# A hybrid encoder layer on one core: a projection moved into the attention stage, and every third low part made in PSUM and copied by ScalarE

## The chip, the cores and the metric

The kernel runs on one core of a Trainium2 chip. Its metric is the device time of one execution in microseconds (us). Three runs of the kernel before took 3136.9, 3138.69 and 3145.14 us; the median is 3138.69. One further execution was profiled. The engines are named as in the profile: PE does matmuls (PEld is its loading of weights), DVE is the vector engine, ACT the scalar engine, POOL GpSimd, SP the engine on whose queue nearly all DMAs are issued.

## The reference

The input `x` is 2048 rows of 1024 numbers in float32. The layer is cut here to its data flow:

```python
h = layer_norm(x) @ w_in                     # 1024 -> 9 x 1024
q, k, v, z_sb, c_val, c_gate, z_cv, g_sb, g_cv = split(h)
o_sb = stick_breaking_attention(q, k, v)     # 16 heads of 64, strictly causal
y_sb = (o_sb * silu(z_sb)) @ w_sb_proj
u = c_val * sigmoid(c_gate)
u = causal_depthwise_conv(u, conv_w) + conv_b        # 31 taps per channel
u = silu(layer_norm(u))
y_cv = (u * silu(z_cv)) @ w_cv_proj
merged = sigmoid(g_sb) * y_sb + sigmoid(g_cv) * y_cv
out = layer_norm(2 ** 0.25 * x + merged @ w_out)
```

The attention's weight of key s for query t is `sigmoid(l_ts)` times the product of `1 - sigmoid(l_tj)` over the keys j between them, so a running product over the keys stands where another attention has a softmax.

## The kernel before, in words

All matmuls that matter run in the type fp32r. A float32 operand is split for them into a high part (an ACT copy to fp32r, L116) and a low part (a DVE subtraction, L117); a product of two split operands takes three matmuls, high by high, high by low and low by high. A tile is 128 partitions by 512 columns (`CH`); the sequence has four chunks of 512, in two halves h = 1 (chunks 3 and 2) and h = 0 (chunks 1 and 0). The rows are reversed on the host, so half 1 is the first half in time of the attention's keys that both need.

There are three phases.

1. **First phase.** The input's layer norm and transposes, and 56 groups of projections by `w_in` (L909), each with seven products instead of eight. `order(h)` sets the groups' order. The groups `u` give the convolution's input; the convolution itself is a queue `slow` of single steps on DVE (its taps are L409). `slow_step` is called once per filling piece. It adds `PACES[phase]` to a balance and, if the balance is at least 1, takes one off and does one step.
2. **Attention stage.** For 8 head pairs, 2 heads and 4 query blocks of 256: two logits matmuls into PSUM (`lg`, L583 and L584), a sigmoid on ACT (`nb`, L586), a running product on DVE (the scan, L589), transposes on PE into a PSUM tile `tp` (L612, `turn`), the split of `tp` into `th` and `tl` (L116 and L117), and products of `v` with `th` and `tl` added up in `pv` (L628). There are 576 such tiles. `weave_attention` writes their order: the `pv` of a tile stands two turns behind its transposes. Between these items stand pieces of filling work, six matmuls each (L201), spread in proportion to the attention's estimated costs: the projections of half 0 for q, k, v and z, and the output projections `branch("s", 1)` (by `w_sb`) and `branch("c", 1)` (by `w_cv`). The convolution's mean and layer norm (`conv_mean`, `conv_ln`, L447 to L505) are delayed entries in the same list of pieces. `END` is how many entries of the list are left for after the attention.
3. **Tail.** `branch("s", 0)`, the output rows of chunks 3 and 2 (L1243), `branch("c", 0)`, the output rows of chunks 1 and 0.

PE's order is the order in which the code is written. On ACT, DVE and SP a scheduler places instructions by priority at build time; each engine then runs its list strictly in order. `tp` has two PSUM buffers, `th` and `tl` two buffers each, `nb` four.

The weights `w_sb` and `w_cv` are loaded and split by `load_w` once for each half. A block's weights are requested during the block before it.

Of the kernel before, what the change touches and what calls it, by code (L numbers as in the profile page):

```python
# [8 lines left out]
F32 = mybir.dt.float32  # L9
# [4 lines left out]
P = 128  # L14
# [16 lines left out]
PACES = [0.78, 1.25, 0.6]  # L31
# [4 lines left out]
END = 14  # L36
W0 = 3
N1 = 2
# [16 lines left out]
def layer_kernel(ctx: ExitStack, tc, x, w_in, w_sb, w_cv, w_out, vecs, cw, rows, out):  # L55
# [15 lines left out]
    nc.gpsimd.memset(ones, 1.0 / D)  # L71
    vec = const.tile([P, 5, KB], F32, name="vec")
# [9 lines left out]

    mhalf = const.tile([P, 1], F32, name="mhalf")
# [60 lines left out]
    def load_w(src, col):  # L144
# [3 lines left out]
        for g in range(2):  # L148
# [7 lines left out]
            split(raw, hi[:, ks], lo[:, ks])  # L156
        return hi, lo
# [282 lines left out]
    def conv_mean(h):  # L440

        def mean(c):
            while len(convs) < (2 - h) * KB:
                slow_step(True)
            ps, mu, ys = mm_p.tile([P, CH], F32, name="mm"), st(), st()
            dma(ys.rearrange("p (e n) -> p e n", e=2), ysd[h][:, :, c % 2 * 256:c % 2 * 256 + 256])
# [3 lines left out]
        return [lambda c=c: mean(c) for c in half(h)]  # L450

    def conv_ln(c):
# [11 lines left out]
        def s2(m):  # L464
# [8 lines left out]
            else:  # L473
                nc.vector.tensor_tensor(out=box["sq"], in0=box["sq"], in1=y, op=ALU.add)

# [4 lines left out]
        def m2():  # L480
            ps = mm_p.tile([P, CH], F32, name="mm")
            for b in range(nb):
                nc.tensor.matmul(ps[:, b:b + 1], lhsT=box["sq"][:, b * P:(b + 1) * P], rhs=ones[:, 0:1], start=True, stop=True)
            v = sm.tile([P, nb], F32, name="var", bufs=2)
            nc.vector.tensor_copy(out=v, in_=ps[:, :nb])
# [3 lines left out]
        def m3():  # L489
            ps = mm_p.tile([P, CH], F32, name="mm")  # L490
            rb = st()
            nc.vector.tensor_copy(out=rb.rearrange("p (b r) -> p b r", b=nb), in_=box["v"].unsqueeze(2).to_broadcast([P, nb, P]))
            for b in range(nb):
                nc.tensor.matmul(ps[:, b * P:(b + 1) * P], lhsT=rb[:, b * P:(b + 1) * P], rhs=ident, start=True, stop=True)
# [14 lines left out]
        return ([m1] + wait + [(lambda m=m: s2(m)) for m in range(KB)] + wait + [m2] + wait + [m3]  # L509
# [3 lines left out]
    def attention(at, kv, lg_p, pv_p):  # L513
# [5 lines left out]
        sums = {}  # L519
# [38 lines left out]
        def make_step(i, a, qc, lo, hi, diag, last, k2, v2, qd, ql, po, prev, load):  # L558
# [39 lines left out]
            for t in range(nt):  # L598
                box = {}

                def turn(t=t, box=box):
# [3 lines left out]
                    for sb in (1, 0):  # L605
                        off = t * 256 + sb * P
                        o0 = at_
                        for j in range(2):
# [3 lines left out]
                            nc.tensor.transpose(out=tp[:, at_:at_ + P], in_=tiles[j][:, so:so + P], identity=ident)  # L612
# [3 lines left out]
                    tl = at.tile([P, CH], F32R, name="tl", bufs=2)  # L616
                    with tc.high_priority(offset=500):
# [700 lines left out]
```

## Time and profile before

| | |
|---|---|
| median of 3 runs | 3138.69 us |
| profiled execution, its own time | 3146.49 us |
| its span, first to last instruction | 3144.7 us |
| mean granted clock of PE | 0.978 |
| PE busy, matmuls | 2896.8 us (92%) x14666 |
| DVE busy | 2603.8 us (83%) x3537 |
| ACT busy | 1414.0 us (45%) x2582 |
| DMA moved | 604.98 MB, 192 GB/s |

Busy time of PE counts the whole duration of a matmul. Matmuls overlap, so their mean duration is longer than the interval between two of them; where PE does nothing else, the interval is read from how many start in 100 us. In rows of groups the columns are: line, engine, operation, output and inputs, shapes and count, busy us and mean ns of one, and idle time of the engine ahead of them with what ended it. In rows of stretches: from and to, length, then for each engine its busy us and count, then the granted clock, the DMA share and GB/s.

### The profile page before, as it was taken

Reading aid. Unit: us, or ns where it says so; the run is one execution under the profiler, and the core shown is the slowest. Engines: PE = TensorE matmul, PEld = TensorE weight load, DVE = VectorE, ACT = ScalarE, POOL = GpSimd, SP = SyncE. Lnnn points to the kernel's source line nnn. Section 1 sums busy time; section 2 is a strip of 40 time slices with the busy share of each in tenths; the row PEclk is TensorE's granted clock in tenths of the full one; section 3 lists DMA queues with packets and bytes.
Section 4 is the critical chain, followed back from the end, with each engine's and each line's share of the span. In section 5 each row is a group of like instructions: output and inputs, shape, how many; then the busy total and the mean of one; then the engine's idle time right before and its main releaser. Section 6 shows DMA issues by size and latency. Waiting matters only on the chain.

```text
span 3144.7 us, 42164 instructions
## 1 busy us (share of the span) xinstructions
PE 2896.8 (92%) x14666; PEld 2402.7 (76%) x14666; DVE 2603.8 (83%) x3537; ACT 1414.0 (45%) x2582; POOL 75.4 (2%) x162
## 2 busy tenths in 40 slices
PE   6998999999999998899889889998899888879998
PEld 4776787878788886787777778887788777767887
DVE  8988989888777865998999988888988898856746
ACT  6553444444422323444454554555645555543322
POOL 1000000000000000000000000000000000000000
PEclk8999999999999999999999999999999999989999
DMA  5878757577865567555563454444543553486552
GB/s 179 301 232 307 264 194 267 206 264 282 286 222 185 176 228 218 169 182 176 182 185 119 149 172 134 156 146 140 167 129 118 158 180 120 145 288 231 169 187 81
DMA packets 319269, 604.98 MB, mean 192 GB/s; under 512 B 37456, under 2 KB 79568, under 8 KB 318928
## 3 DMA queue, kind: packets, MB, share of 16 engines
q1 hardware_dynamic: 319056, 602.29, 58.3%
q8 instruction: 115, 1.88, 0.3%
q14 instruction: 98, 0.80, 0.1%
HBM read 355.74 MB, written 246.42 MB: 191 GB/s over the span
## 4 chain that ended last, share of the span: by engine, by line
PE 47%; DVE 25%; issue 12%; DMA 7%; ACT 3%; SPq 1%; POOL 1%; DVEq 0%; POOLq 0%; ACTq 0%
PE pb L909 11%; PE mm L201 10%; DVE nb L589 10%; PE pp L909 7%; PE mm L909 7%; DVE tl L117 4%; PE tp L612 4%; PE pv L628 3%; PE lg L583 1%; DVE cy L409 1%; PE lg L584 1%; ACT th L116 1%; DVE cu L409 1%; ACT nb L586 1%; DMA st<-fdr 1%
## 5 line engine op out<-in xcount | busy, mean ns | idle before, releaser
L116 ACT ACTIVATE th<-tp 128x512 fp32r<-128x512 f32 (+1 forms) x576 | 329.6, 573 | 467.8 <-PE tp L612 459.2
L117 DVE TENSOR_TENSOR tl<-tp,th 128x512 fp32r<-128x512 f32 (+1 forms) x576 | 374.2, 652 | 92.2 <-ACT th L116 89.1
L612 PE MATMUL tp<-ident,nb 128*128 128x128 f32 x2176 | 354.6, 279 | 80.4 <-DVE nb L589 63.5
L586 ACT ACTIVATE nb<-lg 128x512 f32<-128x512 f32 (+3 forms) x640 | 331.3, 532 | 115.7 <-PE lg L584 114.0
L589 DVE TENSOR_TENSOR_SCAN nb<-nb,dd 128x256 f32<-128x256 f32 (+7 forms) x256 | 343.8, 1348 | 18.0 <-ACT nb L586 18.0
L628 PE MATMUL pv<-tl,v 128*128 128x256 f32 (+1 forms) x1152 | 303.1, 292 | 53.2 <-DVE tl L117 52.5
L612 PEld LDWEIGHTS tp<-ident,nb 128*128 128x128 f32 x2176 | 255.2, 142 | 116.7 <-DVE nb L589 78.8
L589 DVE TENSOR_TENSOR_SCAN nb<-nb,zero 128x1024 f32<-128x1024 f32 x128 | 300.1, 2347 | 23.3 <-ACT nb L586 23.1
L628 PE MATMUL pv<-th,v 128*128 128x256 f32 (+1 forms) x1152 | 307.8, 285 | 2.8 <-ACT th L116 2.6
L583 PE MATMUL lg<-k,qd 128*128 128x512 f32 (+3 forms) x640 | 267.9, 420 | 23.7 <-ACT nb L586 11.7
L628 PEld LDWEIGHTS pv<-tl,v 128*128 128x128 f32 x1152 | 219.1, 190 | 91.7 <-DVE tl L117 76.4
L628 PEld LDWEIGHTS pv<-th,v 128*128 128x128 f32 x1152 | 219.7, 191 | 20.5 <-ACT th L116 4.5
L584 PE MATMUL lg<-k,ql 128*128 128x512 f32 (+3 forms) x640 | 234.7, 367 | 0.0
L201 PE MATMUL mm<-A11h,w 128*128 128x512 f32 x512 | 185.6, 409 | 12.7 <-ACT w L116 7.0
L409 DVE SCALAR_TENSOR_TENSOR cy<-cu,csum,cy 128x512 f32<-128x512 f32 x240 | 179.2, 747 | 18.9 <-ACT cy L405 15.8
L201 PE MATMUL mm<-A12h,w 128*128 128x512 f32 x512 | 188.0, 413 | 0.0
L201 PE MATMUL mm<-SXh,w 128*128 128x512 f32 x512 | 182.8, 403 | 2.1 <-DVE st L712 2.1
L201 PE MATMUL mm<-A22h,w 128*128 128x512 f32 x512 | 182.7, 403 | 0.0
L409 DVE SCALAR_TENSOR_TENSOR cu<-cd,cwt,cu 128x512 f32<-128x512 f32 x240 | 179.1, 746 | 3.7
L409 DVE SCALAR_TENSOR_TENSOR cy<-cu,cwt,cy 128x512 f32<-128x512 f32 x240 | 179.1, 746 | 2.6
L583 PEld LDWEIGHTS lg<-k,qd 128*128 128x128 f32 x640 | 122.5, 191 | 48.7 <-ACT nb L586 29.0
L584 PEld LDWEIGHTS lg<-k,ql 128*128 128x128 f32 x640 | 123.7, 193 | 8.8 <-issue 0.2
(251 smaller groups left out, 6298.9 us busy)
## 6 DMA issues: line engine op xcount, KB each, us to landing
wdr<-w4x SPq DMA_DIRECT2D x78, 512.0 KB, 3.4
wdr<-w SPq DMA_DIRECT2D x68, 512.0 KB, 3.2
w4x<-wdr SPq DMA_DIRECT2D x52, 512.0 KB, 4.7
wraw<-in_w_in SPq DMA_DIRECT2D x100, 256.0 KB, 3.5
w<-wdr SPq DMA_DIRECT2D x96, 256.0 KB, 3.8
k<-kdr SPq DMA_DIRECT2D x192, 128.0 KB, 3.0
v<-vdr SPq DMA_DIRECT2D x96, 256.0 KB, 3.0
w<-wdr SPq DMA_DIRECT2D x46, 512.0 KB, 4.4
```

Of the source, the lines that this page charges most:

```text
L116: nc.scalar.activation(hi, src, AF.Copy)
L117: nc.vector.tensor_tensor(out=lo, in0=src, in1=hi.bitcast(F32), op=ALU.subtract)
L201: nc.tensor.matmul(box["ps"], lhsT=l[:, kb], rhs=r[kb], start=(kb == 0 and n == 0), stop=(kb == KB - 1 and n == 2))
L409: nc.vector.scalar_tensor_tensor(out=dst, in0=src[:, j:j + HN], scalar=t, in1=first, op0=ALU.mult, op1=ALU.add)
L583: nc.tensor.matmul(lg[:, :w], lhsT=qd[c][:, js], rhs=k2[kc][:, ko:ko + w], start=True, stop=False)
L584: nc.tensor.matmul(lg[:, :w], lhsT=ql[c][:, js], rhs=k2[kc][:, ko:ko + w], start=False, stop=True)
L586: nc.scalar.activation(nb[:, o:o + w], lg[:, :w], AF.Sigmoid, scale=-QS)
L589: nc.vector.tensor_tensor_scan(out=nb[:, :w], data0=nb[:, :w], data1=dd[:, :w] if diag else zero.to_broadcast([P, w]), initial=0.0 if diag ...
L612: nc.tensor.transpose(out=tp[:, at_:at_ + P], in_=tiles[j][:, so:so + P], identity=ident)
L628: nc.tensor.matmul(o[:, :w], lhsT=lv, rhs=tt[:, o0:o0 + w], start=(diag and t == 0 and n == 0 and e == 0), stop=(last and t == nt - 1 and ...
L909: nc.tensor.matmul(bank, lhsT=wt[:, e, kb], rhs=xs_[kb][a], start=start and kb == 0 and n == 0, stop=kb == 3 and n == 2, skip_group_check= ...
```

## The change

- **The moved block.** `branch("c", 0)` runs in the attention stage behind `branch("c", 1)`; its partial result is what `branch("s", 0)` adds to in the tail. The convolution's layer norm of half 0 is placed one branch earlier and one entry apart instead of two (`N1`). `END` goes from 14 to 20.
- **Kept weights.** On its first splitting `load_w` writes the parts of `w_sb` and `w_cv` to DRAM (64 writes) and reads them back for half 0.
- **Every third tile.** For each third tile of the attention `split` is left out: ACT makes `th` as before, a matmul adds `-th` onto `tp` in PSUM (`rest`, with the constant `negid`), and ACT copies what remains to `tl`. For this the transposes clear the PSUM bank only with the first of a tile. `rest` stands just ahead of the next tile's transposes.
- **Mean and variance.** Their sums are made by fp32r products of split operands instead of float32 products, and the variance is spread by transposes one slot later. The norm of half 1 gets 13 slots per pair two entries apart, where it had 10 three apart.
- **Order and pace.** `order(h)` puts three other groups behind each `u` of half 1 and one of half 0; before it was 28 and 12 spread evenly over eight. `PACES[1]` goes from 1.25 to 1.6.

```diff
-PACES = [0.78, 1.25, 0.6]
+PACES = [0.78, 1.6, 0.6]
...
-END = 14
+END = 20
...
-N1 = 2
+N1 = 1
...
+    negid = const.tile([P, P], F32R, name="negid")
+    nc.scalar.activation(negid, ident, AF.Copy, scale=-1.0)
...
             split(raw, hi[:, ks], lo[:, ks])
+            if src is not w_in:
+                d = wdr[id(src), col, g] = dram([P, 2, 4, P], F32R, f"wdr{len(wdr)}b")
+                dma(d[:, 0], hi[:, ks])
+                dma(d[:, 1], lo[:, ks])
...
-            nc.tensor.matmul(ps, lhsT=ones, rhs=ys, start=True, stop=True)
+            for c in half(h):
+                ys = st()
+                dma(ys.rearrange("p (e n) -> p e n", e=2), ysd[h][:, :, c % 2 * 256:c % 2 * 256 + 256])
+                parts[c] = st(F32R), st(F32R)
...
+            for n, t in enumerate(parts.pop(c)):
+                nc.tensor.matmul(ps, lhsT=onesr, rhs=t, start=n == 0, stop=n == 1)
...
-                            nc.tensor.transpose(out=tp[:, at_:at_ + P], in_=tiles[j][:, so:so + P], identity=ident)
+                            nc.tensor.matmul(tp[:, at_:at_ + P], lhsT=tiles[j][:, so:so + P], rhs=ident, is_transpose=True,
+                                             start=at_ == 0, stop=True, skip_group_check=True)
...
+                    count[0] += 1
                     with tc.high_priority(offset=500):
-                        split(tp[:, :at_], th[:, :at_], tl[:, :at_])
-                    box["t"] = th, tl
+                        if count[0] % 3:
+                            split(tp[:, :at_], th[:, :at_], tl[:, :at_])
+                        else:
+                            nc.scalar.activation(th[:, :at_], tp[:, :at_], AF.Copy)
+                            box["rest"] = tp, th, tl, at_
+
+                def rest(box=box):
+
+                    if "rest" in box:
+                        tp, th, tl, at_ = box.pop("rest")
+                        nc.tensor.matmul(tp[:, :at_], lhsT=negid, rhs=th[:, :at_], start=False, stop=True, skip_group_check=True)
+                        with tc.high_priority(offset=500):
+                            nc.scalar.activation(tl[:, :at_], tp[:, :at_], AF.Copy)
...
                 if len(queue) == 2:
                     outl.append((n, n, queue.pop(0)))
+                if left:
+                    outl.append((n, n, left.pop()))
+                left.append(rest)
                 outl.append((n, n, turn))
...
-        src, bys = (w_sb, [gate]) if n == "s" else (w_cv, [gate, other])
+        src, bys = w_sb if n == "s" else w_cv, [gate] if n == "sc"[h == 0] else [gate, other]
...
-            us_ = [("u", m) for m in range(KB)]
             rest = [(e, m) for m in range(4) for e in ("kqvzcgh" if h else "cgh")]
+            n = 3 if h else 1
             out_ = []
-            for n, u in enumerate(us_):
-                out_.append(u)
-                out_ += rest[len(rest) * n // 8:len(rest) * (n + 1) // 8]
-            return out_
+            for m in range(KB):
+                out_ += [("u", m)] + rest[m * n:m * n + n]
+            return out_ + rest[KB * n:]
...
+        F.soon([(0.1, it) for it in conv_mean(0) + conv_ln(1) + conv_ln(0)], N0, N1)
         run(F, branch("s", 1), loads("c", 1))
-        F.soon([(0.1, it) for it in conv_mean(0) + conv_ln(1) + conv_ln(0)], N0, N1)
-        run(F, branch("c", 1), loads("s", 0))
+        run(F, branch("c", 1), loads("c", 0))
+        run(F, branch("c", 0), loads("s", 0))
...
         run(F, branch("s", 0), loads("m", 1))
-        output(F, 3, loads("c", 0)[0])
-        output(F, 2, loads("c", 0)[1])
-        run(F, branch("c", 0), loads("m", 0))
+        output(F, 3, loads("m", 0)[0])
+        output(F, 2, loads("m", 0)[1])
         output(F, 1, ())
         output(F, 0, ())
```

What this does to the instructions is seen best in the built orders. First PE, in the second half of the attention stage; `tp` are the transposes of a tile, `lg` the logits, `pv` the products of an earlier tile, and the lines are each kernel's own. Before:

```order
L612 MATMUL tp<-ident,nb 128x128 x3
L583 MATMUL lg<-k_20472,qd 128x512
L584 MATMUL lg<-k_20472,ql_10666 128x512
L628 MATMUL pv<-th,v_20475 128x256
L628 MATMUL pv<-tl,v_20475 128x256
L628 MATMUL pv<-th,v_20475 128x256
L628 MATMUL pv<-tl,v_20475 128x256
L612 MATMUL tp<-ident,nb 128x128 x4
```

Now, at a third tile:

```order
L635 MATMUL tp<-ident,nb 128x128 x4
L606 MATMUL lg<-k_21075,qd 128x512
L607 MATMUL lg<-k_21075,ql_10670 128x512
L665 MATMUL pv<-th,v_21068 128x256
L665 MATMUL pv<-tl,v_21068 128x256
L665 MATMUL pv<-th,v_21068 128x256
L665 MATMUL pv<-tl,v_21068 128x256
L654 MATMUL tp<-th,negid 128x512
L635 MATMUL tp<-ident,nb 128x128 x4
```

The product with `negid` stands between the `pv` of an earlier tile and the next tile's transposes, and it reads the `th` that ACT makes from the transposes at the top.

Second ACT in the same stage, where `nb` is a sigmoid of logits. Before:

```order
L116 ACTIVATE th<-tp 128x512
L586 ACTIVATE nb<-lg 128x128
L116 ACTIVATE th<-tp 128x512
L586 ACTIVATE nb<-lg 128x512
L116 ACTIVATE th<-tp 128x512
```

Now:

```order
L609 ACTIVATE nb<-lg 128x128
L647 ACTIVATE th<-tp 128x512
L609 ACTIVATE nb<-lg 128x512
L656 ACTIVATE tl<-tp 128x512
L120 ACTIVATE th<-tp 128x512
```

A second copy, `tl`, follows the `th` of a third tile with a sigmoid between them, and the next tile's `th` stands behind it.

Third SP, where the tail's first weights of `w_sb` are loaded. Before:

```order
L155 DMA wraw<-in_w_sb 128x512
L93 DMA gt<-gat_2s 128x512
L155 DMA wraw<-in_w_sb 128x512
L1211 DMA raw<-in_w_out 128x1024
L93 DMA pdr_1_173<-st 128x512
```

Now:

```order
L97 DMA st<-asb_7_95 128x512
L97 DMA w_28204<-wdr48b 128x512
L97 DMA w_28205<-wdr48b 128x512
L97 DMA w_28204<-wdr49b 128x512
L97 DMA w_28205<-wdr49b 128x512
```

Where raw weights were read and then split, four DMAs now bring the kept parts straight into the tiles that PE reads.

More of the change, by code (lines that the diff above doesn't have):

```diff
@@ L71, in layer_kernel @@
     nc.gpsimd.memset(ones, 1.0 / D)
+    onesr = const.tile([P, P], F32R, name="onesr")
+    nc.scalar.activation(onesr, ones, AF.Copy)
     vec = const.tile([P, 5, KB], F32, name="vec")
@@ L482, in m2 @@
             for b in range(nb):
[L483 removed]
+                for n, t in enumerate(box["sp"]):
+                    nc.tensor.matmul(ps[:, 2 * b:2 * b + 2], lhsT=t[:, b * P:(b + 1) * P], rhs=onesr[:, 0:2], start=n == 0, stop=n == 1)
             v = sm.tile([P, nb], F32, name="var", bufs=2)
[L485 removed]
+            nc.vector.tensor_copy(out=v, in_=ps[:, :2 * nb].rearrange("p (b e) -> p b e", e=2)[:, :, 0])
             rsqrt_eps(v, v, nb)
@@ L489, in m3, with m4 @@
         def m3():
-            ps = mm_p.tile([P, CH], F32, name="mm")
-            rb = st()
+            box["rb"] = rb = st()
             nc.vector.tensor_copy(out=rb.rearrange("p (b r) -> p b r", b=nb), in_=box["v"].unsqueeze(2).to_broadcast([P, nb, P]))
+        def m4():
+            ps, rb = mm_p.tile([P, CH], F32, name="mm"), box["rb"]
             for b in range(nb):
-                nc.tensor.matmul(ps[:, b * P:(b + 1) * P], lhsT=rb[:, b * P:(b + 1) * P], rhs=ident, start=True, stop=True)
+                nc.tensor.transpose(out=ps[:, b * P:(b + 1) * P], in_=rb[:, b * P:(b + 1) * P], identity=ident)
             box["rs"] = copied(ps)
@@ L508, in conv_ln @@
         wait = [lambda: None] * (W1 if h else W0)
-        return ([m1] + wait + [(lambda m=m: s2(m)) for m in range(KB)] + wait + [m2] + wait + [m3]
+        return ([m1] + wait + [(lambda m=m: s2(m)) for m in range(KB)] + wait + [m2] + wait[1:] + [m3, lambda: None, m4]
                 + [(lambda m=m: s3(m)) for m in range(KB)])
@@ L662, in weave_attention @@
         outl, np_ = [], 0
-        queue = []
+        queue, left = [], []
         pos = 0
-        tile_of = []
         for n, (li, ti) in enumerate(steps):
-            for t, (turn, pv) in enumerate(ti):
+            for t, (turn, pv, rest) in enumerate(ti):
                 while np_ < len(ls):
@@ L678, in weave_attention @@
                 pos += 1
-        return outl + [(n, n, it) for it in queue]
+        return outl + [(n, n, it) for it in left + queue]
     acts = {}
@@ L1160, in layer_kernel @@
         norm = conv_mean(1) + conv_ln(3) + conv_ln(2)
+        slots = [lambda: norm.pop(0)() for _ in norm]
         for i in range(NPAIR):
```

26 lines of the change are left out of this document (16 added, 10 removed).

## The prediction

> **What bounds the kernel now.** I read first the busy time of each engine by stage, cut where the line of the first attention product (L583) begins and where the last `pv` product (L628) ends. The view shows, for each stretch, busy time and instructions of PE, PEld (weight loads), DVE, ACT and POOL, then the granted clock and the DMA share; rows of single 100 us stretches stand below.
>
> ```profile
> 0.00:1192.00 1192.00, 1134.75 (x4927) 917.22 (x4928) 996.98 (x1553) 485.06 (x860) 39.87 (x85) 0.98 0.70 239
> 1192.00:2741.00 1549.00, 1388.56 (x8158) 1183.22 (x8158) 1351.46 (x1595) 801.70 (x1547) 17.62 (x29) 0.98 0.50 157
> 2741.00:3144.70 403.70, 373.45 (x1585) 302.29 (x1583) 255.37 (x389) 127.22 (x175) 17.90 (x48) 0.96 0.57 191
> 2300.00:2400.00 100.00, 99.04 (x580) 85.00 (x579) 78.27 (x87) 46.55 (x89) 0.00 (x0) 1.00 0.44 136
> 2200.00:2300.00 100.00, 86.12 (x511) 73.41 (x510) 92.02 (x108) 61.33 (x116) 0.00 (x0) 0.98 0.49 156
> 1900.00:2000.00 100.00, 92.88 (x557) 79.58 (x557) 80.34 (x88) 50.58 (x99) 1.92 (x3) 1.00 0.47 143
> 2000.00:2100.00 100.00, 93.59 (x564) 79.94 (x562) 87.57 (x96) 54.45 (x105) 0.61 (x3) 1.00 0.44 142
> 900.00:1000.00 100.00, 100.00 (x435) 81.37 (x434) 76.90 (x113) 28.79 (x48) 0.00 (x0) 1.00 0.61 201
> ```
>
> The first phase is PE's: 1135 of 1192 us. The attention stage, half of the program, is nobody's: PE 90%, DVE 87%, ACT 52%, and PE stands idle for 1549.0 - 1388.6 = 160 us. The two neighbouring stretches 2200 and 2300 tell why. They hold the same attention work and a different amount of filling projections:
>
> ```profile
> 2200.00:2300.00 100.00, 23.84 (x146) 17.08 (x146) 0.98 0.49 156
> 2300.00:2400.00 100.00, 22.58 (x147) 17.27 (x147) 1.00 0.44 136
> 2300.00:2400.00 100.00, 53.38 (x204) 36.57 (x204) 1.00 0.44 136
> 2200.00:2300.00 100.00, 33.89 (x125) 22.79 (x124) 0.98 0.49 156
> ```
>
> The first two rows are the transposes of L612, the last two the projection matmuls of L201. With DVE at 92% PE did 146 transposes and 125 fill matmuls and idled for 14 us; with DVE at 78% it did 147 and 204 and idled for 1 us. So where DVE is lighter the same attention work leaves room for 79 more matmuls at no cost in time. The waits of the stage name DVE too; columns are the total in us, the count and the longest:
>
> ```profile
> PE tp L612 <- DVE nb L589: 63.5, 58, 4.4
> PE pv L628 <- DVE tl L117: 52.5, 77, 2.6
> PE tp L612 <- DVE tl L117: 16.3, 14, 2.2
> PE lg L583 <- ACT nb L586: 11.7, 29, 2.6
> PE lg L583 <- DMA k<-kdr: 11.1, 1, 11.1
> ```
>
> 63.5 + 52.5 + 16.3 = 132 us of PE's idle time end on DVE: late scans, late low parts `tl`, and PSUM held by a late `tl`. The tail (404 us) is PE's again, with three kinds of wait in it:
>
> ```profile
> PE mm L201 <- DVE st L712: 7.8, 2, 5.7
> PE mm L201 <- ACT w L116: 7.0, 2, 6.2
> PE mm L483 <- DVE sum L474: 5.8, 1, 5.8
> ```
>
> **The change, part by part.** The price of a 128x512 matmul is its issue interval, not its mean duration: the stretch 900 to 1000 has 435 of them in 100 us of full PE, 0.230 us each.
>
> *A block moved.* The convolution's projection of the first half (`branch("c", 0)`, 384 matmuls) leaves the tail and becomes filling of the attention stage; ten pieces instead of five now remain after the last `pv`. The built orders count 2274 projection matmuls in the stage and 798 after it before, 2628 and 444 now: 354 x 0.230 = 81 us leave the tail and enter the attention stage. Out of the tail goes also the layer norm's rest (the L483 wait, 5.8 us) and the second splitting of `w_sb` and `w_cv`, which is now read back ready made (L116's 7.0 us); the L712 wait (7.8 us) may stay, though DVE has 104 fewer instructions there. After the first of these waits matmuls ran at half rate:
>
> ```profile
> 2753.10 0.39 PE L201 MATMUL mm<-A12h,w 128*128 128x512 f32 x1
> 2759.74 0.80 PE L201 MATMUL mm<-A11h,w 128*128 128x512 f32 x1 [6.25 <-ACT w L116]
> 2760.33 0.63 PE L201 MATMUL mm<-A11l,w 128*128 128x512 f32 x1
> 2760.76 1.05 PE L201 MATMUL mm<-A11h,w 128*128 128x512 f32 x2
> ```
>
> Two starts 0.43 us apart (2760.33, 2760.76) against 0.23; the tail's clock of 0.96 costs 0.04 x 404 = 16 us. Of 20.6 us of waits and 16 us of clock I take 20 us as saved (none to 36). **Tail: -101 us.**
>
> *Every third low part.* 192 of 576 tiles lose their DVE subtraction and get a product with the negative identity and a second ScalarE copy.
>
> ```profile
> L117 DVE TENSOR_TENSOR tl<-tp,th 128x512 fp32r<-128x512 f32 x448 | 304.7, 683 | 85.7 <-ACT th L116 83.2
> L117 DVE TENSOR_TENSOR tl<-tp,th 128x384 fp32r<-128x384 f32 x128 | 69.6, 544 | 6.5 <-ACT th L116 5.9
> L116 ACT ACTIVATE th<-tp 128x512 fp32r<-128x512 f32 x448 | 266.9, 596 | 367.5 <-PE tp L612 361.1 <-DVE nb L589 2.2 <-DVE cy L409 1.5
> L116 ACT ACTIVATE th<-tp 128x384 fp32r<-128x384 f32 x128 | 62.7, 490 | 100.4 <-PE tp L612 98.1 <-PE lg L584 1.6 <-DVE A22l L117 0.2
> ```
>
> The order has 152 tiles of 512 columns and 40 of 384 among them. DVE loses 152 x 0.683 + 40 x 0.544 = 126 us; ACT gains 152 x 0.596 + 40 x 0.490 = 110 us; PE gains 152 x 0.230 + 40 x 0.173 (three quarters) = 42 us. The trace has no accumulating product onto a transpose. From below it costs no less than the 256-column `pv` products, from above 0.31 us, which is what a 512-column product takes just behind transposes (starts 1706.36 and 1706.67 below). I take 0.230, that of its own width; the ends are 23 and 60 us for all.
>
> ```profile
> 1705.98 0.63 PE L612 MATMUL tp<-ident,nb 128*128 128x128 f32 x4
> 1706.36 0.48 PE L201 MATMUL mm<-A12h,w 128*128 128x512 f32 x1
> 1706.64 0.60 ACT L116 ACTIVATE th<-tp 128x512 fp32r<-128x512 f32 x1 [0.25 <-PE tp L612]
> 1706.67 0.39 PE L201 MATMUL mm<-A12l,w 128*128 128x512 f32 x1
> 1707.30 0.67 DVE L117 TENSOR_TENSOR tl<-tp,th 128x512 fp32r<-128x512 f32 x1
> ```
>
> The Trainium skill's page "TensorE: Matmul & The Clock Gate", section "Back-to-back issue gap", gives about 131 ns as the sustained spacing at 512 columns; the row shows 230 ns. By the page the 192 products would cost 25 us, an estimate, and the sum below would be 17 us lower. I go by the row.
>
> *A new wait.* The product stands in PE's queue one place behind its tile's transposes, and everything of PE is queued behind it: first the next tile's transposes. It needs `th`: above, 1706.64 + 0.60 - 1705.98 = 1.26 us from the first transpose to the end of the copy, about 0.9 us after the last one starts. Between them the order has a logits pair and a `pv`, 2 x 0.23 + 4 x 0.12 = 0.94 us, and in most places six fill matmuls (1.38 us) as well. The second hop, product to ACT copy to `pv`, is as long and has as much cover. So a wait where no fill stands between, or a sigmoid (0.60 us) is ahead on ACT. Bounds: nothing; or, for each of 192 tiles, the mean of today's waits for `tl`, 52.5 / 77 = 0.68 us, 131 us. A tile that waits on ACT no longer waits on DVE, and two thirds of the places are covered, so I take 22 us, nearer the low end.
>
> *DVE's balance in the stage.* It loses 126 us and takes over, by the order, 76 instructions of 128x512 (layer norm of the first half, its `c` inputs split, the gating): 76 x 0.683 = 52 us. 1351 - 126 + 52 = 1277 us. ACT goes to some 802 + 110 + 35 = 947 us, about 59%.
>
> *Inert parts.* `PACES[1]` from 1.25 to 1.6 should draw the convolution forward. A call takes at most one step however large the pace, and both values are over 1: the order has 598 taps ahead of the first scan in both, as the trace has:
>
> ```profile
> 0.00:1192.00 1192.00, 444.72 (x598) 0.98 0.70 239
> 1192.00:2741.00 1549.00, 101.70 (x138) 0.98 0.50 157
> ```
>
> So nothing for it. If it worked, 102 us of taps would leave the stage. The other group order in the first phase changes no count there; PE is busy for 95% of it and hides it: 0 us, give or take 10. The mean's and norm's products in another number format are 56 small ones off the path: 0. The 64 new writes of split weights go through SP's queue, DMA share 0.50 in the stage: hidden; where one holds back a load of `k` the price is a wait like the 11.1 us one above, once.
>
> *The sum.* PE gets 81 + 42 = 123 us in a stage with 160 us of idle time. DVE's share falls from 87% to 1277 / 1600 = 80%. In single stretches PE's idle share is 14% at 92% of DVE, 6% at 88%, 7% at 80%, 1% at 78%; I take 4%, 65 us, so 95 us are won back. **Attention stage: 123 - 95 + 22 = +50 us.** All: -101 + 50 + 0 = **-51 us**. The profiled execution took 3146.5 us (span 3144.7), 7.8 above the median 3138.7; -51 on the median is **3088 us**.
>
> **Rivals.** *PE is left no idle time* (chance 0.13). As at 2300 to 2400, 1% idle: 16 of 1530 us, so 144 us are won back, and no new wait: 123 - 144 = -21, with the tail's -117: -138, 3001 us. For it: that stretch. Against: it had ACT at 47%, and the layer norm of the first half is now packed twice as densely into the stage (`N1` 2 to 1).
>
> *PE waits for ScalarE at the new product* (0.17, slower). Its place is the PE queue at every third tile. At 0.68 us each the new waits are 131 us in place of 22: -51 + 109 = +58, 3197 us. It outweighs the rest from 22 + 51 = 73 us on, 0.38 us per changed tile. For it: two hops through an engine that goes from 52% to 59%, and a sigmoid between `th` and `tl` on ACT. Against: ACT ends only 14 us of PE's waits today (11.7, and 2.6 on `th`).
>
> ```profile
> PE pv L628 <- ACT th L116: 2.6, 5, 1.1
> ```
>
> *PE has less to win back* (0.15). Busy time counts a matmul's whole flight, and a short gap disappears in it or is stretched by it; weight loads are short and lie one to a matmul. By them, against the full stretch at 900 (81.37), the stage's 1183.22 us are 1454 us of full PE, and 95 us are idle, not 160. At the same share, 95/160, that gives back 56 us: -51 + 39 = -12, 3127 us. The Trainium skill's page "Perfetto Trace Analysis", section "Identifying the Most-Contended Engine", takes this side: it calls matmul busy time a poor measure and wants the weight loads' share. Against: at 2300, with the stage's own mix of matmuls, the full share is 85.00, which leaves 157 us. For: two thirds of the tiles still go over DVE, behind scans of 2.35 us.
>
> ```profile
> L589 DVE TENSOR_TENSOR_SCAN nb<-nb,zero 128x1024 f32<-128x1024 f32 x128 | 300.1, 2347 | 23.3 <-ACT nb L586 23.1
> ```
>
> **How the numbers follow.** The forecast, with its bounds (tail 81 to 117 saved, 70 to 115 won back, 0 to 45 of new waits, hardly all at one end), has 0.55 and a range of its own of 3055 to 3120. Differences under 0.3% (9 us) can't be told from none here. The third rival lies at that edge and splits into 0.07 faster and 0.08 the same; so faster 0.55 + 0.13 + 0.07 = 0.75, same 0.08, slower 0.17. The range runs from 3035 to 3150: most of the first rival and the greater part of the slower one are left out, about 0.2 together.
>
> **What would show it.** Right: a tail near 300 us; 2628 fill matmuls in an attention stage near 1600 us; DVE about 80% and PE about 95% there; waits of `pv` on `tl` by DVE below 35 us; waits of the new product on ACT below 40 us; 598 taps ahead of the first scan. Wrong: a stage over 1650 us with PE waiting for `th` or for ACT's `tl`; scan waits as large as today's 63.5 us; or a tail that keeps gaps of 6 us.

## The result, and the profile after

The changed kernel takes 3123.7 us (median of 4 runs) against 3141.9 for the kernel before beside it: a ratio of 0.9941, interval 0.9921 to 0.996, or 18 us less. Forecast were 51 us less. The profiled execution has a span of 3122.6 us. By stage, with the columns of the prediction's first fence:

```profile
0.00:1189.00 1189.00, 1132.69 (x4930) 915.63 (x4930) 998.61 (x1553) 485.23 (x862) 40.70 (x85) 0.99 0.70 240
1189.00:2823.00 1634.00, 1508.39 (x8702) 1281.62 (x8701) 1296.63 (x1483) 926.19 (x1784) 21.20 (x30) 0.98 0.56 177
2823.00:3122.60 299.60, 283.28 (x1215) 229.32 (x1213) 190.86 (x285) 82.68 (x106) 17.27 (x47) 0.98 0.55 186
```

The tail shrank from 403.7 to 299.6 us (-104, forecast -101). The attention stage grew from 1549 to 1634 us (+85, forecast +50). PE is busy there for 120 us more (forecast 123), so the miss lies in PE's idle time: 160.4 us before, 1634.0 - 1508.4 = 125.6 us now. 35 us were won back on balance. PE's waits in the stage:

```profile
PE tp L635 <- DVE nb L612: 41.9, 38, 3.4
PE pv L665 <- DVE tl L121: 21.0, 30, 2.5
PE tp L654 <- ACT th L647: 13.7, 16, 3.0
PE lg L606 <- DMA k<-kdr: 11.6, 1, 11.6
PE lg L606 <- ACT nb L609: 11.5, 25, 1.9
PE pv L665 <- ACT tl L656: 7.8, 13, 1.5
...
PE tp L635 <- ACT tl L656: 2.7, 4, 0.7
```

Waits for scans fell from 63.5 to 41.9 us, waits of `pv` for a DVE `tl` from 52.5 to 21.0. New are the rows of L654 and L656: 13.7 + 7.8 + 2.7 = 24 us, forecast 22. The filling products in the stage and behind it, and the two new instructions of a third tile (rows of groups):

```profile
1189.00:2823.00 1634.00, 707.78 (x2628) 479.19 (x2629) 0.98 0.56 177
2823.00:3122.60 299.60, 104.70 (x444) 84.73 (x444) 0.98 0.55 186
...
L654 PE MATMUL tp<-th,negid 128*128 128x512 f32 x152 | 65.4, 430 | 12.7 <-ACT th L647 12.6
L656 ACT ACTIVATE tl<-tp 128x512 fp32r<-128x512 f32 x152 | 90.5, 596 | 95.5 <-PE tp L654 92.7
```

2628 and 444, as the built orders had it. In the tail the three old waits (20.6 us) are gone, and four of another kind stand there, for the kept weights, 6.7 us in all. The longest:

```profile
PE mm L209 <- DMA w<-wdr50b: 4.2, 1, 4.2
```

### The profile page after: what moved, and what is told of

It is laid out like the page before. It is cut to its first block, busy times and chain, and to the rows that moved or that the text cites. A ratio compares the mean times of both kernels' runs of the same rounds, so it can differ in the third digit from the quotient of the medians.

```text
span 3122.6 us, 42554 instructions
## 1 busy us (share of the span) xinstructions
PE 2924.4 (94%) x14842; PEld 2426.6 (78%) x14842; DVE 2486.1 (80%) x3321; ACT 1494.1 (48%) x2752; POOL 79.2 (3%) x162
## 5 line engine op out<-in xcount | busy, mean ns | idle before, releaser
L635 PE MATMUL tp<-ident,nb 128*128 128x128 f32 x2176 | 349.4, 277 | 51.4 <-DVE nb L612 41.9
L121 DVE TENSOR_TENSOR tl<-tp,th 128x512 fp32r<-128x512 f32 (+1 forms) x384 | 249.9, 652 | 131.3 <-ACT th L120 128.7
L635 PEld LDWEIGHTS tp<-ident,nb 128*128 128x128 f32 x2176 | 259.5, 142 | 94.2 <-DVE nb L612 56.4
L209 PE MATMUL mm<-A11h,w 128*128 128x512 f32 x512 | 186.9, 408 | 6.7 <-DMA w<-wdr50b 4.2
L209 PE MATMUL mm<-A12h,w 128*128 128x512 f32 x512 | 188.0, 411 | 0.0
L209 PE MATMUL mm<-SXh,w 128*128 128x512 f32 x512 | 186.2, 408 | 0.0
L209 PE MATMUL mm<-A22h,w 128*128 128x512 f32 x512 | 183.2, 402 | 0.0
L656 ACT ACTIVATE tl<-tp 128x512 fp32r<-128x512 f32 (+1 forms) x192 | 110.1, 574 | 103.1 <-PE tp L654 99.4
```

Of the source, the lines that this page charges most:

```text
L121: nc.vector.tensor_tensor(out=lo, in0=src, in1=hi.bitcast(F32), op=ALU.subtract)
L209: nc.tensor.matmul(box["ps"], lhsT=l[:, kb], rhs=r[kb], start=(kb == 0 and n == 0), stop=(kb == KB - 1 and n == 2))
L635: nc.tensor.matmul(tp[:, at_:at_ + P], lhsT=tiles[j][:, so:so + P], rhs=ident, is_transpose=True, start=at_ == 0, stop=True, skip_group_ch ...
L656: nc.scalar.activation(tl[:, :at_], tp[:, :at_], AF.Copy)
```

## The experiments

Four theories stand in the first expectations. Theory 1: the third tiles are what won back idle time. Theory 2: their road over PE and ACT costs about what DVE's relief brings. Theory 3: half 0's norm, packed twice as densely, takes the gain back. Theory 4: the loop of logits, sigmoid, scan and transposes sets the pace, with no engine full. Later runs take the rest of the change apart. The time is the median of a kernel's runs, and each ratio is against the kernel before on the same chip beside it. The last three columns are of one profiled execution; "idle" is the stage's length less PE's busy time in it.

| kernel | us | ratio (interval) | stage | PE busy | idle |
|---|---|---|---|---|---|
| before | 3141.9 | 1 | 1549 | 1389 | 160 |
| changed | 3123.7 | 0.9941 (0.9921 to 0.996) | 1634 | 1508 | 126 |
| e1, no third tiles | 3107.3 | 0.9890 (0.9874 to 0.9907) | 1619 | 1471 | 148 |
| e2, before with third tiles | 3151.7 | 1.0032 (1.0021 to 1.0042) | 1555 | 1430 | 125 |
| e3, `N1` 2 | 3121.2 | 0.9941 (0.9926 to 0.9955) | 1629 | 1506 | 123 |
| e4, third tiles for nothing | 3067.5 | 0.9770 (0.9756 to 0.9785) | 1573 | 1449 | 124 |
| e5, their product alone | 3104.6 | 0.9881 (0.9855 to 0.9907) | 1609 | 1488 | 121 |
| e6, their copy alone | 3091.6 | 0.9844 (0.9819 to 0.9870) | 1592 | 1453 | 139 |
| e7, no low parts at all | 3030.8 | 0.9647 (0.9628 to 0.9666) | 1534 | 1439 | 95 |
| e8, e1 with lead 5 | 3131.6 | 0.9965 (0.9950 to 0.9979) | 1634 | 1478 | 156 |
| e9, changed with lead 5 | 3158.1 | 1.0043 (1.0027 to 1.0060) | 1660 | 1515 | 145 |
| e10, e1 with lead 4.5 | 3101.9 | 0.9863 (0.9848 to 0.9878) | 1612 | 1470 | 142 |
| e11, e4 with lead 5 | 3098.1 | 0.9854 (0.9835 to 0.9874) | 1606 | 1471 | 135 |
| e12, e1 without kept weights | 3094.9 | 0.9836 (0.9821 to 0.9850) | 1611 | 1463 | 148 |
| e13, e12 with lead 4.5 | 3098.3 | 0.9841 (0.9821 to 0.9861) | 1615 | 1473 | 142 |
| e14, changed without kept weights | 3110.8 | 0.9887 (0.9872 to 0.9903) | 1626 | 1502 | 124 |
| e15, before with the moved block alone | 3122.0 | 0.9919 (0.9901 to 0.9937) | 1638 | 1478 | 160 |
| e16, e12 with even filling | 3093.1 | 0.9828 (0.9805 to 0.9851) | 1613 | 1469 | 144 |
| e17, e12 with the old group order | 3096.4 | 0.9849 (0.9829 to 0.9868) | 1611 | 1461 | 150 |
| e18, before with the new norm alone | 3155.4 | 1.0038 (1.0026 to 1.0051) | 1547 | 1390 | 157 |

Five runs fell outside every range that was expected of them: e7, e8, e9, e12 and e18; e10 missed by less than 1 us.

### The third tiles

e1 takes them out of the changed kernel, e2 puts them alone into the one before.

```diff
-                        if count[0] % 3:
+                        if True:
```

> The changed kernel with every low part made by DVE again; all else stays. Theory 1 (the low parts on ScalarE are what won back idle time in the stage): DVE's work in the attention stage rises by 126 us to 1423, PE's falls by 42, PE's waits for DVE go back from 67 to about 132 us, so the stage grows by about 132 - 67 - 42 - 24 (the new waits on ACT go) = -1 to +30 us; the time is 3123 to 3155. Theory 2 (the product and its two hops cost PE about as much as the relief brings, and the gain is the moved block alone): the stage shortens, 3095 to 3123.

> The kernel before with the third low part on ScalarE alone; the block is not moved. Theory 1: the stage had 160 us of idle PE, DVE falls from 87% to about 80%, 66 us of waits on DVE go and 42 us of products and 24 us of new waits come: about 0, 3125 to 3142. Theory 2: the product is paid on PE without filling work to spend the relief on: 3142 to 3165.

Without them the changed kernel is faster by 0.9941 - 0.9890 = 0.51%, 16 us; alone they cost the kernel before 0.32%, 10 us. For e2 the edit is the change's own part on every third tile, with the transposes that clear the bank once and `rest`'s place in the weaving; e1 keeps these two. e4 to e6 take it apart. In e4 a third tile has no low part: no subtraction, no product, no second copy, and `pv` reads the high part twice, so that PE's other work stays and part of the computation is missing. e5 keeps the product with `negid`, e6 the second copy.

```diff
-                            box["rest"] = tp, th, tl, at_
+                            box["t"] = th, th
```

> Every third tile's low part is left out: no subtraction, no product, no second copy; its products read the high part twice, so PE's products with v are as many as before. This leaves out part of the computation. It shows what the route over PE and ACT costs, with DVE's relief kept. By the sum: 42 us of products and 24 us of waits on ACT go, 3123 - 66 = 3057. If PE's slack covers the products (theory 4, the loop sets the pace): 3100 or more.

For e5, where `pv` reads the high part twice as well, and so again a part of the computation is left out:

```diff
+                            box["t"] = th, th
...
-                            nc.scalar.activation(tl[:, :at_], tp[:, :at_], AF.Copy)
```

> The changed kernel without the second ScalarE copy: the product with the negative identity is made and read by nobody, the tile's products take the high part twice (part of the computation is left out). Between this and the kernel with every third tile free (3067.5) lies the product alone with its wait for the high part. If the issue interval is the price (42 us of products and 14 us of waits): 3115 to 3125, and the copy with its hop costs nearly nothing. If the second hop and the copy weigh as much as the product: 3090 to 3105.

For e6, whose `tl` is then a second copy of the high part:

```diff
-                        nc.tensor.matmul(tp[:, :at_], lhsT=negid, rhs=th[:, :at_], start=False, stop=True, skip_group_check=True)
```

> The changed kernel without the product: ScalarE copies the transposed tile itself a second time, and that copy stands in for the low part (part of the computation is changed). Between this and the kernel with every third tile free (3067.5) lies the 110 us of work on ScalarE alone. If ScalarE has room and the price is PE's: 3065 to 3078. If ScalarE's load delays sigmoids and high parts: 3085 to 3105.

Stage of e1 and of e4:

```profile
1189.00:2808.00 1619.00, 1470.52 (x8509) 1258.78 (x8509) 1399.67 (x1675) 835.29 (x1592) 18.25 (x30) 0.97 0.56 179
```

```profile
1191.00:2764.00 1573.00, 1448.63 (x8510) 1244.21 (x8509) 1292.56 (x1483) 832.53 (x1592) 19.30 (x30) 0.98 0.57 184
```

Taking 192 subtractions from DVE, 1399.7 - 1292.6 = 107 us of its busy time, brings 3107.3 - 3067.5 = 40 us; `pv`'s wait for these low parts goes with them. In the two profiled executions the stage is 46 us shorter: PE's idle time falls by 24 us, and its busy time by 22 with the same number of matmuls. The product costs 3104.6 - 3067.5 = 37 us (with PE's busy time up by 39; the forecast's price was 42), the copy 24, and both together 3123.7 - 3067.5 = 56. So theory 2 holds: 56 for 40, 16 us lost. Of theory 1 the idle time holds: the third tiles take it from 148 us (e1) to 126, and in e2 from 160 to 125. But they add 38 and 41 us to PE's busy time. Theory 4 expected 3100 us or more of e4; that did not come. Where the copy's 24 us arise is seen in PE's waits for scans, first in e4 and then in e6:

```profile
PE tp L635 <- DVE nb L612: 58.5, 50, 5.2
...
PE tp L635 <- DVE nb L612: 73.5, 54, 5.2
```

They grow by 15 us, as PE's idle time does (124 to 139). That the copies delay the sigmoids on ACT, and these the scans, is the likely reason, but not shown. In e7 no tile has a low part.

```diff
-                        if count[0] % 3:
-                            split(tp[:, :at_], th[:, :at_], tl[:, :at_])
-                        else:
-                            nc.scalar.activation(th[:, :at_], tp[:, :at_], AF.Copy)
-                            box["rest"] = tp, th, tl, at_
+                        nc.scalar.activation(th[:, :at_], tp[:, :at_], AF.Copy)
+                        box["t"] = th, th
```

> No tile has a low part at all: no subtraction on DVE, no product, no copy; the products with v read the high part twice (part of the computation is left out). DVE loses 374 us against the changed kernel without the third part (3107.3), to about 65% of the stage. If PE's remaining idle time comes from DVE's load in proportion (40 us for the first 126): 3107 - 119 = 2988. If it is DVE's fill of its queue that decides and the first third took the most: 3040 to 3055. If the loop logits, sigmoid, scan, transposes sets the pace (latency): 3050 to 3067.

Twice as many subtractions more leave DVE, 1292.6 - 1080.1 = 212 us, and bring only 3067.5 - 3030.8 = 37 us. Stage and waits of e7, the waits being PE's and then DVE's own:

```profile
1195.00:2729.00 1534.00, 1439.21 (x8510) 1245.56 (x8511) 1080.11 (x1099) 830.82 (x1593) 20.58 (x30) 0.98 0.59 188
...
PE tp L635 <- DVE nb L612: 61.5, 46, 3.7
...
DVE nb L612 <- ACT nb L609: 244.7, 177, 7.5
```

With DVE at 1080 of 1534 us, 70%, PE still waits 61.5 us for scans, as long as in the kernel before with 87%. DVE in turn stands idle for 245 us ahead of scans until a sigmoid is done. These scan waits are not DVE's load.

### The norm's density and the lead

> The changed kernel with the layer norm of half 0 two entries apart again (N1 = 2). Theory 3 (what remains idle on PE sits where DVE is locally full, 2100 to 2500, at 83 to 88%, because the norm is packed twice as densely there): spread over double the length that stretch loses about 10% of DVE and PE's idle share there falls from 11% to 6%, 15 to 20 us: 3103 to 3110. Theory 4 (it is the loop of latencies logits, sigmoid, scan, transposes, with no engine full): no change, 3119 to 3128.

`N1` back to 2 changes nothing (0.9941 both): theory 3 falls. The lead is how many tiles the logits are written ahead of their transposes (`LEAD`, 4.0 in both kernels).

```diff
-LEAD = 4.0
+LEAD = 5.0
```

> The changed kernel without the third part (3107.3), and the logits written five tiles ahead of their transposes instead of four (LEAD 4 to 5; the number of buffers stays). If scans come late because their logits are issued late (latency of the loop), PE's 70 us of waits for scans fall by a third or more: 3070 to 3090. If scans come late because DVE is busy or blocked in its list, or the buffers bound the lead: 3100 to 3115.

> The changed kernel with the logits written five turns ahead of their transposes in place of four (LEAD 5); nothing else. With every low part on DVE this lead cost 24 us (3107 to 3132): scan waits fell from 70 to 10 us and waits for tl rose from 31 to 78. Theory A (with lead 5 the wait is for DVE's subtraction, since scans then stand ahead of it; the third tiles give DVE room and so pay here): faster than 3123.7, about 3095 to 3115, with waits of pv on DVE's tl under 40 us. Theory B (the third tiles' road over PE and ACT costs its 16 us with any lead): 3130 to 3150. In the middle, 3115 to 3130, neither.

> The changed kernel with every low part on DVE and a lead of 4.5 turns. Lead 4 took 3107.3 us, lead 5 took 3131.6. If scan waits and waits for tl trade off smoothly with the lead, between the two: 3105 to 3125, scan waits between 10 and 70 us. If half a turn only moves a few logits (they are written at whole turns), the same as one of its neighbours within 5 us.

> Lead 5, and the third tiles have no low part at all (no subtraction, no product, no second copy; their pv reads the high part twice, so a part of the computation is left out). With lead 4 this took 3067.5 us, 40 less than with every low part on DVE, of 126 us taken from DVE. If the lead was what kept DVE's relief from paying (at lead 4 PE waits 58 us for scans that a lighter DVE does not hasten): under 3050, that is 80 us or more below the 3131.6 of lead 5 with every low part on DVE. If relief pays its 40 us whatever the lead: about 3090. Between: both.

PE's waits in e8, which answer to 69.6 us for scans and 31.3 for `tl` in e1:

```profile
PE pv L665 <- DVE tl L121: 78.1, 86, 2.9
PE lg L606 <- ACT nb L609: 21.4, 41, 2.6
...
PE tp L635 <- DVE nb L612: 10.1, 9, 3.2
```

A longer lead does away with most of the scan waits and gives as much back as waits for low parts: with the rows for L635 and L312, which are not shown, they go from 49 us in e1 to 107 in e8, and waits for sigmoids from 15.6 to 21.4. That DVE keeps its order, and an earlier scan then stands ahead of a subtraction, is the likely reason; no row here shows it. I took from this that relief of DVE pays with lead 5. It does not: the third tiles make e9 slower than e8 by 0.78%, 25 us, and the free ones make e11 faster than e8 by 1.1%, 35 us, no more than the 40 at lead 4. Half a tile of lead makes no difference that holds: 0.27% faster with the kept weights (e10), 0.05% slower without (e13).

> The changed kernel with every low part on DVE, without the kept weights, and a lead of 4.5 turns. With lead 4 this took 3094.9 us; the half turn of lead brought 5 us with the kept weights. If the two are separate: 3085 to 3095. If the half turn's 5 us were of the kept weights or of the measurement: 3093 to 3100.

### The kept weights

```diff
-            if src is not w_in:
+            if False:
```

> The changed kernel with every low part on DVE, and without the kept weights: w_sb and w_cv are loaded raw and split again for half 0, as before the change; no writes of split weights to DRAM. If reading the kept parts back is what took the 7 us wait for a weight's split and the half rate behind it out of the tail, as the prediction had it: 3112 to 3125 against 3107.3, with a tail 7 to 20 us longer and a wait of a matmul on a weight's split in it. If the moved block alone did it: 3102 to 3112.

> The changed kernel without the kept weights alone: the third tiles stay on PE and ACT, w_sb and w_cv are split again for half 0. If the kept weights cost the 12 us (18 by the ratios) that they cost with every low part on DVE, because the tail's start waits for twice the bytes: 3106 to 3113, tail near 290 us. If the splits that come back to ACT collide with the third tiles' copies: 3115 to 3130, with the attention stage longer than 1640 us.

They cost 0.54% with every low part on DVE and 0.54% with the third tiles, 17 us each time. The first 100 us of the tail in the changed kernel:

```profile
2823.00:2873.00 50.00, 44.23 (x182) 35.25 (x181) 26.29 (x35) 15.77 (x22) 0.00 (x0) 0.93 0.84 281
2873.00:2923.00 50.00, 49.09 (x217) 40.29 (x216) 17.46 (x23) 6.01 (x6) 0.00 (x0) 1.00 0.91 315
```

The same in e12:

```profile
2804.00:2854.00 50.00, 49.94 (x222) 41.41 (x223) 34.45 (x51) 22.89 (x33) 0.00 (x0) 1.00 0.86 300
2854.00:2904.00 50.00, 50.00 (x222) 41.42 (x221) 24.63 (x35) 12.43 (x17) 0.00 (x0) 1.00 0.83 283
```

182 + 217 matmuls with the kept weights (187 + 203 in e1, which differs from e12 by the kept weights alone), 222 + 222 without: 45 fewer, 10 us at 0.230. A kept block is two parts to read where a raw one is one, and PE waits for their arrival, 6.7 us of the 10; DMA is about equally busy in both. DVE and ACT have room for the splitting: in e12 they are busier by 15 and 14 us in these 100 us, and PE is not held. e12's whole tail is 3094.2 - 2804 = 290 us, 12 shorter than e1's 302, and its stage 8 us shorter.

### The block, the norm and the order

e15 is the kernel before with the moved block alone (`branch("c", 0)` in the stage, the norm's place, `N1`, `END`). e17 is e12 with the old `order`. Against e15 it has the new mean and variance, and three things more: the transposes that clear the bank once, an empty `rest` entry for each tile in the weaving, and the pace. e18 is the kernel before with only the new mean and variance.

```diff
-        run(F, branch("s", 1), loads("c", 1))
         F.soon([(0.1, it) for it in conv_mean(0) + conv_ln(1) + conv_ln(0)], N0, N1)
-        run(F, branch("c", 1), loads("s", 0))
+        run(F, branch("s", 1), loads("c", 1))
+        run(F, branch("c", 1), loads("c", 0))
+        run(F, branch("c", 0), loads("s", 0))
```

> The kernel before with only the moved block (branch c of half 0 in the attention stage, the norm's place, END 20, N1 1): no kept weights, no third tiles, the old products for mean and variance, the old order of groups. If the moved block is all that gains, this equals the changed kernel without third tiles and kept weights: 3085 to 3105. If mean, variance or the order of groups (priced at nothing in the prediction) carry part of it: over 3105; if they cost: under 3085.

> The changed kernel with every low part on DVE and without the kept weights, and with the old order of groups in the first phase: the moved block and the new mean and variance remain. The moved block alone took 3122 us, with the new order and the new mean and variance 3094.9. If mean and variance carry the 27 us between: 3090 to 3102. If the order of groups does: 3112 to 3125.

> The kernel before with only the new mean and variance (fp32r products of split operands, the spread by transposes one slot later, the norm of half 1 in 13 slots two entries apart). If they take 27 us out of the attention stage wherever the block stands: 3112 to 3122 against 3142. If they pay only beside the moved block, because the norm of both halves is then packed into one stretch: 3130 to 3145. The prediction priced them at nothing.

e15's stage, and the largest of PE's waits there:

```profile
1195.00:2833.00 1638.00, 1477.98 (x8523) 1263.45 (x8522) 1405.79 (x1683) 841.49 (x1600) 21.23 (x30) 0.97 0.52 164
...
PE tp L612 <- DVE nb L589: 72.9, 56, 3.9
PE pv L628 <- DVE tl L117: 40.4, 48, 3.0
...
PE mm L447 <- DMA st<-ysd: 4.0, 2, 3.4
PE mm L494 <- DVE st L492: 3.9, 1, 3.9
```

The block alone gives 0.81%, 25 us, and wins back nothing in the stage: PE's idle time is 160 us, as before it, and the stage is longer by the 89 us that PE is busy longer. (By the weight loads' share, against 81.37 in 100 us, the idle time goes from 95 to 85 us.) The tail is 3123.2 - 2833 = 290 us, without kept weights and without the old wait for a split. With the new mean and variance beside it, and the three things more (e17), it gives 1.51%, 22 us more. In the profiled executions the stage is 27 us shorter: 10 are idle time (160 to 150; the two waits of L447 and L494 in e15, 7.9 us, have no successor in e17) and 17 busy time, at a granted clock of 0.98 in place of 0.97. The two waits and 5 us of the busy time are the mean's and variance's own; for the rest no run parts them from the transposes and the empty entries, which shift the filling. The pace does nothing. The new order of groups (e12 against e17) can't be told from nothing. But the new mean and variance alone (e18) cost 0.38%, 12 us. The stage is as before; PE's waits in the tail, and the last product of each norm step on DVE in the tail (L522; in the kernel before it is L505):

```profile
PE mm L203 <- DVE st L729: 23.3, 5, 9.3
PE mm L498 <- DVE st L729: 5.9, 1, 5.9
...
2740.00:3153.00 413.00, 9.11 (x13) 0.95 0.59 199
```

```profile
2741.00:3144.00 403.00, 5.63 (x8) 0.96 0.58 191
```

The norm has more slots now, and without the moved block 13 of its last steps fall into the tail instead of 8. PE waits there 29 us for the gating of its products (L729), which stands on DVE among them; in the kernel before that was 7.8 us (L712). So edits that I had put down at nothing are not nothing: e18's cost 12 us where they stand alone, and e17's gain 22 together.

### How evenly the filling lies

In e12 the second half of the stage has between 114 and 240 filling matmuls to 36 tiles, since the list is spread by the number of its entries, and an entry of the norm brings no matmul. e16 spreads it by the entries' costs; then it is 156 to 168.

```diff
-            at_fill = max(at_fill, lo + int((hi - lo) * k / work[p_]))
+            while at_fill < end and done_cost[at_fill + 1] <= lo + (hi - lo) * k / work[p_]:
+                at_fill += 1
```

> The changed kernel with every low part on DVE and without kept weights (3094.9 us), and the filling spread over the attention by the pieces' costs in place of their number: a norm's entry counts as a piece but brings no matmul, so the list spreads 114 to 240 fill matmuls on each 36 tiles in the second half; by cost it is 156 to 168. Everything else the same. Theory A (PE's idle time in the stage is the attention's chain of logits, sigmoid, scan, transposes and split left uncovered where the filling is thin): the stage's idle time falls from 148 us to 100 to 130 and the time to 3060 to 3085. Theory B (the idle time is DVE's load, the mean of which stays): 3090 to 3105.

No change: 0.9828 against 0.9836, idle 144 against 148. That PE idles because the filling is thin falls too. With the filling even, though, the trace shows where the idle time is. Four stretches of e16; then the filling of L209 and the norm's products on DVE (L524) in the same four:

```profile
2200.00:2300.00 100.00, 83.71 (x467) 70.24 (x467) 88.71 (x109) 54.26 (x99) 1.02 (x1) 0.93 0.59 191
2300.00:2400.00 100.00, 87.20 (x502) 73.49 (x501) 91.74 (x115) 60.56 (x110) 1.01 (x1) 0.97 0.63 199
2500.00:2600.00 100.00, 96.77 (x581) 83.59 (x580) 86.93 (x96) 49.97 (x95) 0.00 (x0) 1.00 0.47 144
2700.00:2800.00 100.00, 97.75 (x583) 84.45 (x582) 81.75 (x85) 49.58 (x94) 0.00 (x0) 1.00 0.22 72
...
2200.00:2300.00 100.00, 38.02 (x137) 0.93 0.59 191
2500.00:2600.00 100.00, 47.57 (x180) 1.00 0.47 144
...
2200.00:2300.00 100.00, 5.44 (x8) 0.93 0.59 191
2300.00:2400.00 100.00, 4.82 (x7) 0.97 0.63 199
2500.00:2600.00 100.00, 0.00 (x0) 1.00 0.47 144
2700.00:2800.00 100.00, 0.00 (x0) 1.00 0.22 72
```

DVE's share is nearly the same at 2200 (89%) and at 2500 (87%), PE's idle time is 16 and 3 us. What differs is the norm: its steps stand in the first two stretches and in none of the last two. The DMA's share differs too (0.59 and 0.63 against 0.47 and 0.22), and the stretch from 2400 to 2500 does not fit: one such step, DVE at 82%, and 11 us idle. Waits for scans from 2200 to 2500, and then from 2500 to the stage's end:

```profile
PE tp L635 <- DVE nb L612: 29.1, 15, 7.0
...
PE tp L635 <- DVE nb L612: 2.9, 5, 1.5
```

The longest of them, with DVE's timeline ahead of it (start, duration, line, and in brackets what it stood idle for):

```profile
2288.49 0.68 DVE L528 TENSOR_TENSOR st<-st 128x512 f32<-128x512 f32 x1
2291.36 0.69 DVE L484 TENSOR_TENSOR st<-st,mu 128x512 f32<-128x512 f32 x1 [2.19 <-DMA st<-ydr]
2291.97 2.02 DVE L612 TENSOR_TENSOR_SCAN nb<-nb,dd 128x896 f32<-128x896 f32 x1
...
2294.04 0.69 PE L635 MATMUL tp<-ident,nb 128*128 128x128 f32 x2 [6.96 <-DVE nb L612]
```

A subtraction of the norm (L484) waits 2.19 us for a DMA, and the scan that PE needs stands behind it in DVE's list. So a step that is small in DVE's busy time can hold PE by its place: 2.19 us of idle DVE and the step's own 0.69 stand ahead of the scan, out of PE's 6.96. This is one wait of one execution; that most of the scan waits come so is argued from the stretches, and no run moved the norm's steps behind the scans.

## Why the prediction was right and wrong

- **Tail, -101: right as a sum (-104), wrong in its parts.** The 354 moved matmuls are there. But of the 20 us of waits and clock, part was put to the kept weights, which were to do away with the 7.0 us wait for a split. The moved block alone does away with all three waits (e15, tail 290 us), and the kept weights bring their own (4.2 us, and 45 matmuls fewer in 100 us). The writes, priced as hidden, and the reads, not priced at all, cost 17 us together.
- **Third tiles: their prices right.** Product 42 forecast, 37 measured; new waits 22 forecast, 24 seen. The prediction's balance for DVE, 1277 us and 80%, came out at 1297 and 79%. What failed is what its relief is worth.
- **Won back, 95: the step that failed.** The prediction said that "where DVE is lighter the same attention work leaves room for 79 more matmuls at no cost in time", from two neighbouring stretches, and drew a line from DVE's share to PE's idle share. On balance 35 us were won back, 59 with the new waits added; the third tiles alone win as much (160 to 125 us in e2). The moved block won back nothing (160 to 160 in e15), so its 354 matmuls cost their full time; taking 107 us from DVE brought 40 (e4), the next 212 brought 37 (e7). The line took 4% of idle time at 80% of DVE, where its own stretch at 80% had 7%; measured were 7.7% at 79%. And it was drawn through four chosen stretches, while the stage as a whole had 10% at 87%. Two more stretches of the same trace lie far from it:

```profile
1300.00:1400.00 100.00, 90.20 (x530) 77.78 (x531) 96.28 (x128) 47.91 (x99) 1.16 (x2) 0.98 0.53 169
1800.00:1900.00 100.00, 87.88 (x510) 74.40 (x509) 84.83 (x97) 54.87 (x102) 0.00 (x0) 0.98 0.54 176
```

  PE idled 10 us at 96% of DVE and 12 us at 85%. From the stretch at 2200 to the one at 2300 its idle time falls by 0.94 us for each us of DVE; a straight line through all fifteen stretches from 1200 to 2700 us gives 0.35, with much scatter. The two stretches differed in more than DVE's share: in the first stood 18 instructions of the norm on DVE, in the second none. The rows of one of the norm's three lines, L501, in the kernel before:

```profile
2200.00:2300.00 100.00, 4.07 (x6) 0.98 0.49 156
2300.00:2400.00 100.00, 0.00 (x0) 1.00 0.44 136
```

- **Inert parts: right for the pace and the order, wrong for mean and variance.** Pace: 598 taps stand ahead of the first scan, and the built order with the old pace is the same on every engine. Order: nothing (e17). Mean and variance: I counted 56 small products and saw no path; alone they cost 12 us (e18), and beside the moved block they are part of a gain of 22 (e17).
- **The sum.** Measured against the kernel before by ratios: block -25, mean and variance with the new transposes and the empty entries -22, order -4 (within nothing), kept weights +17, third tiles +16, together -18. Two of the misses, these 22 and the kept weights' 17, nearly cancel. The tail's sum was met in part by luck: the block alone saves 113 us there (403.7 to 290.2 in e15), and the kept weights give back 12. The miss of 33 us is about that of the stage, +85 for +50.
- **Rivals.** "PE has less to win back" gave 3127 us, the nearest figure, with 56 us won back where 59 were. Its rule took the weight loads' share as the measure: by 81.37 for 100 us of full PE the idle time went from 95 to 1634 - 1281.62 / 0.8137 = 59 us, 36 won back; by busy time it was 35. So the two measures agree on what was won. But in e7 the rule leaves 1534 - 1245.56 / 0.8137 = 3 us of idle time, while PE's waits in that stage add up to 94 us. With 81.37 it counts too little here, and that its figure came near is luck as far as these runs show. The Trainium skill's page "Perfetto Trace Analysis", section "Identifying the Most-Contended Engine", holds the weight loads' share, with the share of peak arithmetic, for a better measure of the distance from PE's limit than matmul busy time; in e7, 3 us against 94, it is not the better one. "PE waits for ScalarE" (131 us of new waits) and "PE is left no idle time" fall with 24 us of new waits and 126 of idle time.

What stays open: what the 142 to 160 us of idle time hang on in all kernels with every low part on DVE, and which of e17's edits bring its 22 us. The first is not the amount of filling (e15), not its evenness (e16), hardly the lead (e8, e10), and DVE's load only at 0.2 to 0.4 us per us.

The kernel to keep is the change without third tiles and kept weights (e12, 0.9836, or e16, 0.9828): it beats both.

## What to carry to other kernels

A correlation between one engine's load and another's idle time, read from neighbouring stretches, is no price for relief: look first which other instructions stand in the one stretch and not in the other, and where they stand in the in-order list. Filling added to a stage with 10% of idle time need not use any of it (160 us before and after the moved block alone). And weigh a saved computation against the bytes that replace it at the place where they are read: splitting again on engines with room was cheaper than reading twice the bytes while PE waited.

## What the runs showed of the hardware

- A product can be accumulated onto float32 transposes in PSUM; it costs about 0.2 us each (37 us for 192 of them, 152 of 512 columns and 40 of 384), near the 0.230 us between plain products of 512 columns.
- Moving 192 subtractions from DVE to ACT as copies (e6 with the copy, e1 without) gains 16 us; only the product that makes such a copy possible turns it into a loss. The copy itself, off PE, costs 24 of the 40 us gained.
- At the start of the tail, transfers at 281 and 315 GB/s, 84 and 91% of the DMA engines, went with 182 and 217 matmuls of PE in 50 us each; in e12 300 and 283 GB/s went with 222. So the DMA's load alone does not tell how PE is held; with the kept weights PE's waits there were for the kept parts (6.7 us).
